# Attention's transposed exponentials in the projections' PSUM banks, and the values' eviction divided between two engines

## The chip, the core and the metric

The kernel runs on one core of a Trainium2 chip. Five engines work side by side, each through its own instructions in order, and wait for each other by semaphores: TensorE (PE), VectorE (DVE), ScalarE (ACT), GpSimd (POOL) and SyncE (SP), which issues the DMAs of the weights. Matmuls write to PSUM, which has eight banks of 512 float32 per partition; a result is brought from there to SBUF by DVE or ACT ("evicted"). The metric is the device time of one execution in microseconds, as the median of the runs; a smaller one is better.

## The reference, cut to what matters

Two transformer layers with recurrent mixers and mixtures of experts come first, and then one layer of attention and a convolutional MLP. The change touches the attention alone, which works on 256 tokens of width 1024 in 16 heads of 64:

```python
def second_block(x, ...):
    y = rms_norm_2(h, attn_norm[i])
    qkv = (y @ w_qkv[i]).reshape(B, S, 3, N_HEADS, HEAD_DIM)
    ...
    o = moba_attention(q, k, v, rel_bias)
    h = h + o.transpose(0, 2, 1, 3).reshape(B, S, D) @ w_o[i]
    y = rms_norm_2(h, ffn_norm[i])
    h = h + conv_ffn(y, ...)

def moba_attention(q, k, v, rel_bias):     # 256 tokens are one block, the block of all queries
    s_own = jnp.einsum('bhqd,bhkd->bhqk', qi, k_own) * scale
    s_own = s_own + rel_bias[:, rel_bucket(qpos[:, None] - kpos_own[None, :])]
    s_own = jnp.where(kpos_own[None, :] <= qpos[:, None], s_own, NEG)
    p = jax.nn.softmax(...)
    out = jnp.einsum('bhqk,bhkd->bhqd', p, v_own)
```

## The kernel before, in words

**Precision.** Every large float32 product is made of three products in a faster float32 format: weights and activations are split into a high and a low part (high times high, high times low, low times high; lines 346, 347 and 348 in the helper `mm3`). `split_w` makes the two parts of a piece of 128 x 1024 weights: ACT copies the high part (line 297), DVE subtracts it (line 298). Three buffers hold such pieces (`wsp`), so a piece can be split only when TensorE is done with the one three before it.

**PSUM.** The eight banks stand in two pools of four, `acc` and `aux` (lines 168 to 174). A pool hands out its banks in turn, in the order in which the program text asks for them: the fifth request waits until the bank of the first is free again.

**Attention (lines 1279 to 1355).** `proj_T` takes one `acc` bank and computes two feature tiles of q or k for all 256 tokens: 96 matmuls per pair of q and k, in four pieces of weights. The two projections of the first pair are asked for ahead (line 1279). Then the rows' root mean squares are found (`rms_rows`, ACT line 1265 and the DVE lines 454 to 464) and spread over the partitions by a matmul with ones (`rms_cols`, DVE line 1272, PE line 1274, DVE line 1275). A loop runs over four groups of four heads. In each, DVE evicts q and k (line 1300); PE computes the scores of two heads into two `aux` banks, and of two more into two others (line 1308); DVE adds the bias and finds the maxima (lines 1317, 1319); ACT takes exponentials with their sums (line 1321), DVE inverts the sums (line 1322), ACT scales (line 1324); PE transposes the three 128 x 128 blocks of each head into one `aux` bank (line 1331), and ACT or DVE copies them out (line 1334). So a group asks for two `acc` banks and eight `aux` banks.

After the loop `proj_tok` computes v in two halves of 512 columns, each as two token tiles in two `acc` banks (48 matmuls of 512 columns); ACT evicts both tiles with the rows' scale (line 1345); PE multiplies the probabilities by v (line 1352); the output projection `token_out` follows, and then the MLP, in which TensorE is busy to the end.

**Order.** The text is not the order of the engines. A scheduler sets it when the kernel is built: it takes, for each engine, the work that is free by its own estimate, and can take later work first, as far as data and the turns of the banks and buffers allow. At run time each engine keeps the order that was built.

Of the kernel before, what the change touches and what calls it, by code (L numbers as in the profile page):

```python
# [14 lines left out]
AF = mybir.ActivationFunctionType  # L15
OP = mybir.AluOpType
# [28 lines left out]
def two_layer_mixer_moe_then_attention_kernel(  # L45
# [9 lines left out]
    nc = tc.nc  # L55
# [11 lines left out]
    def slab(dt=F32):  # L67
        mem["act"] += 1
        assert mem["act"] + mem["wts"] <= SLOTS, mem
        t = big.tile([P, 2048], dt, tag="slot", name="slab")  # L70
        return t
# [4 lines left out]
    def tok(t):  # L76
        return t[:, :2048].rearrange("p (t d) -> p t d", t=2)
# [90 lines left out]
    def acc():  # L168
        b = psp.tile([P, 512], F32, tag="acc", name="acc")
        return b  # L170

    def aux():
        b = psp.tile([P, 512], F32, tag="aux", name="aux")
        return b
# [25 lines left out]
    def wa(n=512):  # L200
        return ring("a", n)
# [4 lines left out]
    def two(t):  # L206
        return t.rearrange("p (a b) -> p a b", a=2)
# [117 lines left out]
    def split_part(h, l, src):  # L325
        hi = nc.scalar.activation(h, src, AF.Copy)  # L326
        nc.vector.tensor_sub(l, src, h.bitcast(F32))  # L327
        return hi
# [38 lines left out]
    def proj_T(xh, xl):  # L367
        lo_last = len(early) > 1
        if len(early) == 1 and not tr[1:]:
            tr.append(0)  # L370
            wl_last = 1
        else:
            wl_last = 0
        ws = early.pop() if early else split_unit()
        pb = acc()
        for f in range(2):
            wh, wl = next(ws)
            o = pb[:, f * S:(f + 1) * S]
            if f < lo_last:
                mm = None  # L380
                for i, (w, x) in enumerate(((wh, xh), (wl, xh), (wh, xl))):
                    for k in range(8):
                        with tc.issue_after(mm.ins) if mm is not None else ExitStack():
                            mm = nc.tensor.matmul(o, w[:, k, :], x[:, k, :], start=i + k == 0, stop=i == 2 and k == 7)
                last[:] = [mm]
                continue
            if wl_last or lo_last:
                for k in range(8):
                    nc.tensor.matmul(o, wh[:, k, :], xh[:, k, :], start=k == 0, stop=False)
                    mm = nc.tensor.matmul(o, wh[:, k, :], xl[:, k, :], start=False, stop=False)  # L390
                for k in range(8):
                    with tc.issue_after(mm.ins):
                        mm = nc.tensor.matmul(o, wl[:, k, :], xh[:, k, :], start=False, stop=k == 7)
                last[:] = [mm]
                wl_last = 0
                continue
            for k in range(8):
                mm3(o, wh[:, k, :], wl[:, k, :], xh[:, k, :], xl[:, k, :], k == 0, k == 7)
        used()
        return pb  # L400

    def proj_tok(xh, xl):
        outs = [acc(), acc()]
        for hf in range(2):
            unit = take()
            for kp in range(2):
                wh, wl = split_w(unit[:, 2 * kp:2 * kp + 2, :])
                for k in range(2):
                    kk = 4 * hf + 2 * kp + k
                    for t in range(2):  # L410
                        mm3(outs[t], xh[:, kk, t * P:(t + 1) * P], xl[:, kk, t * P:(t + 1) * P],
                            wh[:, k, :], wl[:, k, :], kk == 0, kk == 7)
            used()
        return outs
# [846 lines left out]
    def rms_rows(h, eps=1e-6):  # L1261
        ss = tiny.tile([P, 2], F32, tag="ss", name="ss")
        y = tok(slab())
        for t in range(2):
            nc.scalar.activation(y[:, t, :], h[:, t, :], AF.Square, accum_out=ss[:, t:t + 1])
        drop()
        return [rsqrt(ss[:, t:t + 1], 1.0 / D, eps, 1) for t in range(2)]
# [12 lines left out]
    rs = rms_rows(h0)  # L1280
# [12 lines left out]
    v = tok(slab())  # L1293
    sm = tiny.tile([P, 16, 2], F32, tag="v32", name="asm", bufs=4)
    eT = []
    for a in range(4):
        qT, kT = (two(qk[:, 1024 * (a % 2) + 512 * j:1024 * (a % 2) + 512 * j + 512]) for j in range(2))
        for dst, sc in ((qT, 0.125), (kT, 1.0)):
            pb = ahead.pop(0) if ahead else proj_T(xh, xl)
            nc.vector.scalar_tensor_tensor(dst, two(pb), sc, rbb, op0=OP.mult, op1=OP.mult)  # L1300
        pes = []
        for f in range(2):
            pair = [aux(), aux()]
            for qs_, ks_, os_ in ((slice(0, 128), slice(0, 128), slice(0, 128)),
                                  (slice(128, 256), slice(0, 256), slice(128, 384))):
                for j in range(2):
                    rs_ = slice(64 * j, 64 * j + 64)
                    nc.tensor.matmul(pair[j][:, os_], qT[rs_, f, qs_], kT[rs_, f, ks_], start=True, stop=True)  # L1308
            for j in range(2):
                hi, pb = 2 * f + j, pair[j]  # L1310
                pe = wa(384)
                mx = tiny.tile([P, 2], F32, tag="amx", name="amx")
                tb = table[a // 2][:, 4 * (a % 2) + hi, :]
                rc = sm[:, 4 * a + hi, :]
                blocks = ((0, slice(0, 128), tb[:, 128:256]), (1, slice(128, 384), tb))
                for t, cs, bias in blocks:
                    nc.vector.tensor_tensor_reduce(out=pe[:, cs], in0=pb[:, cs], in1=bias, scale=1.0,
                                                   scalar=-3.0e38, op0=OP.add, op1=OP.max, accum_out=mx[:, t:t + 1])
                nc.vector.tensor_scalar(mx, mx, -1.0, None, op0=OP.mult)
                for t, cs, _ in blocks:  # L1320
                    nc.scalar.activation(pe[:, cs], pe[:, cs], AF.Exp, bias=mx[:, t:t + 1], accum_out=rc[:, t:t + 1])
                nc.vector.reciprocal(rc, rc)
                for t, cs, _ in blocks:
                    nc.scalar.activation(pe[:, cs], pe[:, cs], AF.Copy, scale=rc[:, t:t + 1])
                pes.append(pe)
        for hi in range(4):
            if len(eT) % 5 == 0:
                es = slab()
            pT = aux()
            for b in range(3):  # L1330
                nc.tensor.transpose(pT[:, b * P:(b + 1) * P], pes[hi][:, b * P:(b + 1) * P], ident)
            o = 384 * (len(eT) % 5)
            eT.append(es[:, o:o + 384])
            (nc.vector.tensor_copy if hi % 2 else nc.scalar.copy)(eT[-1], pT[:, :384])
# [7 lines left out]
    for c in range(2):  # L1342
        pbs = proj_tok(xh, xl)
        for t in range(2):
            nc.scalar.activation(v[:, t, 512 * c:512 * c + 512], pbs[t], AF.Copy, scale=rs[t])
        for a in (2 * c, 2 * c + 1):
            po = two(aux())
            for f in range(2):
                for n, r0, ks in ((0, 0, slice(0, 256)), (1, 128, slice(256, 384))):
                    for j in range(2):  # L1350
                        h = 4 * a + 2 * f + j
                        nc.tensor.matmul(po[64 * j:64 * j + 64, f, r0:], v[:, n, 64 * h:64 * h + 64], eT[h][:, ks],
                                         start=n == 0, stop=n == 1)
            split_part(uh[:, 2 * a:2 * a + 2, :], ul[:, 2 * a:2 * a + 2, :], po)
# [22 lines left out]
    pbs = [aux() for _ in range(4)]  # L1377
# [148 lines left out]
```

## Time and profile before

| | us |
|---|---|
| median of 3 runs | 1487.66 (1486.57 to 1487.93) |
| the profiled execution | 1489.95 |
| its span, first to last instruction | 1488.2 |
| PE busy in the span | 1285.9 |
| DVE busy | 551.6 |
| ACT busy | 386.9 |

The profiled execution is 0.15% above the median. The experts of the first two layers wait for their weights; the attention lies between about 1182 and 1266 us of the span, behind the last expert. A busy time is the sum of what an engine's instructions took. Matmuls overlap, so that the length of a run of matmuls is read from start to start, not from a single one's duration.

### The profile page before, as it was taken

What the parts mean: (1) busy time and instruction counts of PE and PEld (TensorE: products, weight loads), DVE (VectorE), ACT (ScalarE), POOL (GpSimd) and SP (SyncE); (2) the same over time, 40 slices, a digit from 0 to 9 for tenths busy, and PEclk for the clock granted to TensorE, in tenths of its full rate; (3) what the DMA queues carried; (4) which work ended last, traced back from release to release, by engine and by line L of the source; (5) the groups of instructions that cost most, each with busy time, mean ns of one, the idle gap of its engine ahead of it and who ended that gap; (6) DMA issues with size and microseconds to landing.
All of it is one profiled execution on the core that took longest, in us unless ns stands there. A gap on an engine that the chain in (4) does not pass through costs nothing.

```text
span 1488.2 us, 27004 instructions
## 1 busy us (share of the span) xinstructions
PE 1285.9 (86%) x11695; PEld 898.2 (60%) x11695; DVE 551.6 (37%) x1145; ACT 386.9 (26%) x637; POOL 104.5 (7%) x84
## 2 busy tenths in 40 slices
PE   9999976666667668999996769999998899999997
PEld 8887633222222226888662426656664797899996
DVE  5774211111001004886410110210100865687776
ACT  5552200000000001754210000000000467465554
POOL 1000002100100000100000210000002400010000
PEclk9999988678667789999997766876769999999999
DMA  9967999999999999847899999999999934655500
GB/s 284 374 227 293 416 420 420 421 422 421 396 421 421 420 421 358 288 172 270 340 420 421 420 413 421 420 420 421 421 421 388 357 122 136 212 191 192 178 28 29
DMA packets 129302, 492.41 MB, mean 331 GB/s; under 512 B 11570, under 2 KB 68037, under 8 KB 81056
## 3 DMA queue, kind: packets, MB, share of 16 engines
q1 hardware_dynamic: 127216, 489.93, 83.9%
q8 instruction: 92, 1.51, 0.4%
q0 software_dynamic: 864, 0.66, 0.2%
q10 hardware_dynamic: 1104, 0.10, 0.1%
q14 instruction: 26, 0.21, 0.0%
HBM read 489.61 MB, written 1.05 MB: 330 GB/s over the span
## 4 chain that ended last, share of the span: by engine, by line
PE 49%; DMA 45%; DVE 3%; POOL 1%; issue 1%; ACT 1%; SPq 0%; DVEq 0%; ACTq 0%; POOLq 0%
DMA unit<-in_moe_w_down_dram 16%; DMA unit<-in_moe_w_up_dram 15%; DMA unit<-in_moe_w_gate_dram 12%; PE acc L347 8%; PE acc L346 8%; PE acc L348 8%; PE acc L976 5%; PE aux L1220 4%; PE aux L1023 2%; PE aux L346 1%; PE aux L347 1%; PE aux L348 1%; DMA unit<-in_w_qkv_dram 1%; PE aux L1308 1%; PE aux L628 1%
## 5 line engine op out<-in xcount | busy, mean ns | idle before, releaser
L976 PE MATMUL acc<-unit,slab 128*32 128x256 f32 x3840 | 315.6, 470 | 108.2 <-DMA unit<-in_moe_w_up_dram 54.1
L976 PEld LDWEIGHTS acc<-unit,slab 128*32 128x32 f32 x3840 | 129.6, 128 | 287.9 <-DMA unit<-in_moe_w_up_dram 88.0
L347 PE MATMUL acc<-slab 128*128 128x256 f32 (+1 forms) x896 | 276.6, 309 | 1.2 <-DVE slab L327 0.8
L348 PE MATMUL acc<-slab 128*128 128x256 f32 (+1 forms) x896 | 276.1, 310 | 0.0
L346 PE MATMUL acc<-slab 128*128 128x256 f32 (+1 forms) x896 | 272.6, 310 | 2.8 <-ACT slab L326 2.8
L298 DVE TENSOR_TENSOR slab<-unit,slab 128x1024 fp32r<-128x1024 f32 x156 | 198.0, 1278 | 67.5 <-ACT slab L297 65.6
L297 ACT ACTIVATE slab<-unit 128x1024 fp32r<-128x1024 f32 x152 | 159.6, 1058 | 144.1 <-PE acc L347 73.2
L1023 PE MATMUL aux<-unit,w 128*32 128x256 f32 x1920 | 152.9, 452 | 44.0 <-DMA unit<-in_moe_w_down_dram 32.8
L346 PEld LDWEIGHTS acc<-slab 128*128 128x128 f32 x896 | 170.9, 191 | 13.7 <-ACT slab L326 3.3
L347 PEld LDWEIGHTS acc<-slab 128*128 128x128 f32 x896 | 171.2, 191 | 12.3 <-issue 2.1
L348 PEld LDWEIGHTS acc<-slab 128*128 128x128 f32 x896 | 171.6, 191 | 9.2 <-issue 1.3
L992 DVE TENSOR_TENSOR w<-w,acc 128x256 f32<-128x256 f32 x32 | 13.5, 421 | 364.2 <-PE acc L976 352.8
L1035 ACT COPY slab<-aux 32x256 f32<-32x256 f32 x60 | 21.7, 361 | 424.3 <-PE aux L1023 423.4
L1023 PEld LDWEIGHTS aux<-unit,w 128*32 128x32 f32 x1920 | 62.2, 124 | 111.2 <-DMA unit<-in_moe_w_down_dram 53.7
L1035 DVE COPY slab<-aux 32x256 f32<-32x256 f32 x60 | 25.4, 424 | 226.2 <-ACT slab L1035 225.8
L1220 PEld LDWEIGHTS aux<-slab 33*128 33x128 f32 x512 | 90.3, 272 | 13.9 <-issue 13.9
L1220 PE MATMUL aux<-slab 33*128 33x16 f32 x512 | 92.6, 328 | 0.0
L991 ACT ACTIVATE w<-acc 128x256 f32<-128x256 f32 x32 | 12.3, 383 | 275.8 <-PE acc L976 275.8
L931 PEld LDWEIGHTS aux<-slab 128*128 128x128 f32 x192 | 30.5, 204 | 8.6 <-issue 7.8
L931 PE MATMUL aux<-slab 128*128 128x128 f32 (+1 forms) x192 | 35.3, 327 | 0.0
L347 PE MATMUL aux<-slab 128*128 128x512 f32 x88 | 34.3, 390 | 0.0
L348 PE MATMUL aux<-slab 128*128 128x512 f32 x88 | 34.2, 389 | 0.0
(338 smaller groups left out, 1198.9 us busy)
## 6 DMA issues: line engine op xcount, KB each, us to landing
unit<-in_moe_w_gate_dram SPq DMA_DIRECT2D x128, 1024.0 KB, 19.8
unit<-in_moe_w_up_dram SPq DMA_DIRECT2D x128, 1024.0 KB, 19.8
unit<-in_moe_w_down_dram SPq DMA_DIRECT2D x128, 1024.0 KB, 19.8
unit<-in_w_up_dram SPq DMA_DIRECT2D x22, 1024.0 KB, 5.6
unit<-in_gla_w_in_dram SPq DMA_DIRECT2D x12, 1024.0 KB, 11.9
unit<-in_w_qkv_dram SPq DMA_DIRECT2D x12, 1024.0 KB, 11.7
unit<-in_mlstm_w_in_dram SPq DMA_DIRECT2D x11, 1024.0 KB, 13.6
unit<-in_w_down_dram SPq DMA_DIRECT2D x11, 1024.0 KB, 4.9
```

The lines of the kernel that those rows point to most:

```text
L297: nc.scalar.activation(h, src, AF.Copy)
L298: eng.tensor_tensor(l, src, h.bitcast(F32), op=OP.subtract)
L346: nc.tensor.matmul(o, ah, bh, start=first, stop=False)
L347: nc.tensor.matmul(o, ah, bl, start=False, stop=False)
L348: last[:] = [nc.tensor.matmul(o, al, bh, start=False, stop=stop)]
L628: mm = nc.tensor.matmul(o, E[d][:, h, o0:o0 + P], v[s][:, h, :], start=i == 0, stop=i == len(terms) - 1)
L931: nc.tensor.matmul(o, n_cols(t, k), ohf[:, t], start=t == 0, stop=t == 1)
L976: mm = nc.tensor.matmul(pb[32 * j:32 * j + 32, :256], picked(kk, e), unit[:, k, 256 * j:256 * j + 256], start=kk == 0, stop=kk == 7)
L1023: mm = nc.tensor.matmul(py[32 * j:32 * j + 32, :256], hT[:, kk % 2, 32 * (kk // 2):32 * (kk // 2) + 32], unit[:, k, 256 * j:256 * j + 256] ...
L1035: eng(yb[32 * eg:32 * eg + 32, g % 2, 256 * j:256 * j + 256], py[32 * j:32 * j + 32, :256])
L1220: nc.tensor.matmul(pb[:, 16 * j:16 * j + 16], cb[:, 256 - c:384 - c], relT, start=True, stop=True)
L1308: nc.tensor.matmul(pair[j][:, os_], qT[rs_, f, qs_], kT[rs_, f, ks_], start=True, stop=True)
```

## The change

The four transposes of a group go to banks of the pool `acc`, which the projections of q, k and v use, and the pool `aux` is left to the scores in this loop: a group now asks for six `acc` banks and four `aux` banks. The eviction of v is divided: the first token tile stays on ACT, the second is scaled by DVE.

```diff
@@ -1326,7 +1326,7 @@
         for hi in range(4):
             if len(eT) % 5 == 0:
                 es = slab()
-            pT = aux()
+            pT = acc()
             for b in range(3):
                 nc.tensor.transpose(pT[:, b * P:(b + 1) * P], pes[hi][:, b * P:(b + 1) * P], ident)
             o = 384 * (len(eT) % 5)
@@ -1342,7 +1342,10 @@
     for c in range(2):
         pbs = proj_tok(xh, xl)
         for t in range(2):
-            nc.scalar.activation(v[:, t, 512 * c:512 * c + 512], pbs[t], AF.Copy, scale=rs[t])
+            if t:
+                nc.vector.tensor_scalar(v[:, t, 512 * c:512 * c + 512], pbs[t], rs[t], None, op0=OP.mult)
+            else:
+                nc.scalar.activation(v[:, t, 512 * c:512 * c + 512], pbs[t], AF.Copy, scale=rs[t])
         for a in (2 * c, 2 * c + 1):
             po = two(aux())
             for f in range(2):
```

Lines behind the second edit stand three further down in the changed kernel (the product with v is line 1355). The scheduler builds another order from the changed text. On TensorE, at the scores of the first group of heads, there stood before (L1308 are scores, L346 to L348 a projection; the projection around them is the first of the third group):

```order
L346 MATMUL acc<-slab 128x256
L347 MATMUL acc<-slab 128x256
L348 MATMUL acc<-slab 128x256
L1308 MATMUL aux<-slab 128x128 x2
L1308 MATMUL aux<-slab 128x256 x2
L1308 MATMUL aux<-slab 128x128 x2
L1308 MATMUL aux<-slab 128x256 x2
L346 MATMUL acc<-slab 128x256
L347 MATMUL acc<-slab 128x256
```

And at the same scores now (L1274 spreads the root mean squares, L1331 are the transposes; the projection ahead of L1274 is the second of all, the one behind L1331 the third):

```order
L346 MATMUL acc<-slab 128x256
L347 MATMUL acc<-slab 128x256
L348 MATMUL acc<-slab 128x256
L1274 MATMUL aux<-w_8239,ones 128x128 x2
L1308 MATMUL aux<-slab 128x128 x2
L1308 MATMUL aux<-slab 128x256 x2
L1308 MATMUL aux<-slab 128x128 x2
L1308 MATMUL aux<-slab 128x256 x2
L1331 MATMUL acc<-ident,slab 128x128 x10
L346 MATMUL acc<-slab 128x256
L347 MATMUL acc<-slab 128x256
```

Ten of the twelve transposes of a group have moved up to stand right behind its scores, and the projections of the following groups, which stood between and around them, have moved behind them; the same holds in all four groups. The two last transposes stand 18 matmuls further on.

On DVE, ahead of the reductions of a group's scores (L1317, L1319), there stood before, at the first group:

```order
L298 TENSOR_TENSOR slab<-unit,slab 128x1024
L464 SCALAR_TENSOR_TENSOR rs_y<-rs_q,rs_y 128x1
L1272 TENSOR_SCALAR w_8239<-ident,rs_y 128x128
L298 TENSOR_TENSOR slab<-unit,slab 128x1024
L1275 COPY slab<-aux 128x256
L1300 SCALAR_TENSOR_TENSOR slab<-acc,slab 128x512 x3
L298 TENSOR_TENSOR slab<-unit,slab 128x1024
L1300 SCALAR_TENSOR_TENSOR slab<-acc,slab 128x512
L298 TENSOR_TENSOR slab<-unit,slab 128x1024
L1317 ISA slab,amx<-aux,slab 128x128
```

And now, at the second group (the third and the fourth are alike):

```order
L1334 COPY slab<-acc 128x384
L298 TENSOR_TENSOR slab<-unit,slab 128x1024
L1300 SCALAR_TENSOR_TENSOR slab<-acc,slab 128x512
L298 TENSOR_TENSOR slab<-unit,slab 128x1024 x2
L1300 SCALAR_TENSOR_TENSOR slab<-acc,slab 128x512
L298 TENSOR_TENSOR slab<-unit,slab 128x1024
L1317 ISA slab,amx<-aux,slab 128x128
```

The eviction of k (the second L1300) now stands one piece of weights ahead of the group's reductions instead of a group ahead of them, and the low part of a later group's weights (the last L298) stands between the two.

## Rows read from the trace of the kernel before

**Rows 1.** The page's slices: PE's busy tenths, and its granted clock in tenths.
```profile
PE   9999976666667668999996769999998899999997
PEclk9999988678667789999997766876769999999999
```

**Rows 2.** Attention's stretch: us, busy (instructions) of PE, PEld, DVE, ACT, POOL; PEclk; DMA; GB/s.
```profile
1182.10:1266.40 84.30, 81.78 (x569) 69.33 (x567) 56.17 (x155) 57.63 (x137) 9.97 (x8) 1.00 0.45 156
```

**Rows 3.** Timeline of PE, ahead of the scores: start, us, line, shapes, count, [idle before, releaser].
```profile
1176.59 0.28 PE L348 MATMUL acc<-slab 128*128 128x256 f32 x1
...
1187.39 0.28 PE L348 MATMUL acc<-slab 128*128 128x256 f32 x1
1189.03 0.49 PE L1274 MATMUL aux<-w,ones 128*128 128x128 f32 x2 [1.37 <-DVE rs_y L455]
1189.28 0.36 PE L346 MATMUL acc<-slab 128*128 128x256 f32 x1
```

**Rows 4.** Timeline of DVE, from the last root mean square to the first reductions.
```profile
1189.86 1.23 DVE L298 TENSOR_TENSOR slab<-unit,slab 128x1024 fp32r<-128x1024 f32 x1
1191.00 0.15 DVE L464 SCALAR_TENSOR_TENSOR rs_y<-rs_q,rs_y 128x1 f32<-128x1 f32 x1
1191.19 0.29 DVE L1272 TENSOR_SCALAR w<-ident,rs_y 128x128 f32<-128x128 f32 x1
...
1192.53 0.43 DVE L1275 COPY slab<-aux 128x256 f32<-128x256 f32 x1
1192.99 1.89 DVE L1300 SCALAR_TENSOR_TENSOR slab<-acc,slab 128x512 f32<-128x512 f32 x3
...
1196.85 1.22 DVE L298 TENSOR_TENSOR slab<-unit,slab 128x1024 fp32r<-128x1024 f32 x1 [0.24 <-ACT slab L297]
1198.00 0.28 DVE L1317 CUSTOM_DVE_ANT_0 slab<-aux,slab 128x128 f32<-128x128 f32 x1
...
1198.55 0.28 DVE L1317 CUSTOM_DVE_ANT_0 slab<-aux,slab 128x128 f32<-128x128 f32 x1
```

**Rows 5.** Timeline of ACT, a piece's high part and one group's exponentials.
```profile
1195.76 1.06 ACT L297 ACTIVATE slab<-unit 128x1024 fp32r<-128x1024 f32 x1 [1.81 <-PE acc L347]
...
1199.31 0.40 ACT L1321 ACTIVATE slab<-slab,amx 128x128 f32<-128x128 f32 x1 [1.18 <-DVE amx L1319]
...
1201.08 0.79 ACT L1324 ACTIVATE slab<-slab,asm 128x128 f32<-128x128 f32 x2
1201.78 1.04 ACT L297 ACTIVATE slab<-unit 128x1024 fp32r<-128x1024 f32 x1
...
1206.12 0.46 ACT L1334 COPY slab<-aux 128x384 f32<-128x384 f32 x1
```

**Rows 6.** Timeline of PE: scores, six transposes, the product with v, 512-column matmuls.
```profile
1196.85 1.58 PE L1308 MATMUL aux<-slab 64*128 64x128 f32 x16
...
1258.43 0.82 PE L1331 MATMUL aux<-ident,slab 128*128 128x128 f32 x6
...
1260.70 5.68 PE L1352 MATMUL aux<-slab 128*64 128x256 f32 x64 [1.15 <-ACT slab L1345]
...
1266.32 0.50 PE L346 MATMUL acc<-slab 128*128 128x512 f32 x1
...
1266.88 0.39 PE L348 MATMUL acc<-slab 128*128 128x512 f32 x1
...
1268.27 0.39 PE L348 MATMUL acc<-slab 128*128 128x512 f32 x1
```

**Rows 7.** Timeline of PE in the first layer, 512-column matmuls behind a wait.
```profile
105.02 0.50 PE L346 MATMUL acc<-slab 128*128 128x512 f32 x1 [2.11 <-ACT slab L326]
...
107.73 1.91 PE L348 MATMUL acc<-slab 128*128 128x512 f32 x4
109.43 0.59 PE L346 MATMUL acc<-slab 128*128 128x512 f32 x1
```

**Rows 8.** A stretch of the first layer, columns as in Rows 2.
```profile
106.45:109.86 3.41, 3.41 (x10) 2.48 (x8) 3.41 (x6) 1.22 (x3) 0.00 (x0) 0.50 1.01 425
```

## Prediction, before the changed kernel was run

> **What bounds the kernel now.** I read the page's slices first, then the attention's stretch, then single instructions in it. In the slices the reader is to see that TensorE is busy to 90% or more in nearly every slice from the last fifth of the span on, at the full clock (2.4 GHz of the two levels 1.2 and 2.4) [rows 1]. The attention lies in that part. In its 84.2 us, from the end of the second projection (1182.1) to the first matmul of the output projection (1266.3), TensorE is busy for 81.8 us, while DVE and ACT have some 27 us each to spare and the DMA is at 0.45 [rows 2]. TensorE waits there only twice: 1.37 us for the root mean squares [rows 3] and 1.15 us for ACT's eviction of v [rows 6]. So TensorE's own work bounds this stretch. The softmax of each group of heads costs no time now because projections of later groups stand between a group's scores and its transposes. Behind the attention TensorE is busy to the end, so what is lost or won here reaches the end.
>
> **The change part by part.** No instruction is added or taken away but for two evictions of v that pass from ACT to DVE. What moves is the order. The two `acc` requests of the next group's q and k now come behind four requests for transposes, and the four banks of the pool go round in turn; a projection can no longer be taken ahead of the transposes of the group before it. In the order that is built, TensorE gets scores, ten transposes, and only then the next projection, four times. Its matmuls start in order: at 1189.03 it had idled 1.37 us for one matmul, and a projection's matmul that needs nothing from that one started only behind it [rows 3]. So each softmax now stands open on TensorE. I add up the new stretch from 1182.1 on.
>
> *Wait for the root mean squares.* Matmuls of 256 columns follow each other at (1187.39 - 1176.59)/90 = 0.12 us [rows 3]; the 46 of them that still stand ahead of line 1274 end at 1182.1. Before, 105 more matmuls filled the time to the scores. Now TensorE waits. On DVE the last step of the root mean square stood behind a low part of 1.14 us (1189.86 to 1191.00), which is gone from there: it starts near 1190.0, line 1272 0.19 later, done at 1190.5; the matmul takes some 0.4 (an estimate from its 0.49 for a pair), the copy 0.46 to the next instruction, two evictions 1.89/3 = 0.63 each [rows 3, 4]. The scores start at 1192.7: **10.6 us**.
>
> *First group.* From the scores' start to the first reduction 0.95 (half of 1.58 [rows 6] and a hand-over); from there to the first exponential 0.86 (1.31 for two heads, 1198.00 to 1199.31, less one head's 0.55 and 0.1 more for the maxima taken singly [rows 4, 5]). Then ACT is the chain: up to the first block of the last head it has four heads of exponentials at (1201.08 - 1199.31)/2 = 0.885, three scalings at 0.70, half a scaling at 0.4 and one copy at 0.46 [rows 5], together 6.5. With 0.2 for the last transpose and 0.3 because these scores would run at the lower clock after the long wait: **8.8 us** to the next projection.
>
> *Groups two to four.* Each begins with 96 matmuls at 0.12 and two transposes, 11.8 us (0.82 for six [rows 6]). Then the next scores need k's eviction (0.2 and 0.68, which a group's distance hid before), and they and half of themselves would put the first reduction 1.85 us behind the projection. But the low part of a later group's weights now stands ahead of the reductions on DVE, and it needs the buffer that the last matmuls free: high part on ACT, low part on DVE, 1195.76 to 1198.00 = 2.24 [rows 4, 5], with 0.2 to release. I take 2.45, the later of the two. Then 1.31 to the first exponential for two heads, 6.5 on ACT, 0.2: 10.45 us, in which TensorE has 2.6 us of scores and transposes. Three groups of 11.8 + 10.45 make **66.7 us**.
>
> *v and the product with it.* 96 matmuls of 512 columns at (1268.27 - 1266.88)/6 = 0.232, two transposes 0.25, the product 1260.70 to 1266.32 = 5.62 [rows 6]: **28.1 us**. The eviction of v in halves costs nothing in this sum: the order puts 20 matmuls of v's second half (4.6 us) between its first half and the product, more than an eviction of some 0.65 on either engine (DVE's nearest row is 0.63 each, line 1300 [rows 4]) and a piece of weights queued ahead of it. If that cover is gone, the 1.15 us of before [rows 6] come back; it can give no more than these, and they are counted as gone already.
>
> Sum: 1182.1 + 10.6 + 8.8 + 66.7 + 28.1 = 1296.3, against 1266.3 before: **30.0 us** more. The four softmaxes and the first wait leave TensorE idle for some 40 us. Against that stand the 2.5 us of the old waits and about 7 us that the old order lost by changing between projections, scores and transposes at many places: its 84.2 us less 2.5 of waits are 81.7, and the same work in the new order adds up to 114.2 - 40 = 74.
>
> *The clock.* The trace has no wait of 7 us between bursts of full matmuls. The nearest one is 2.11 us long (to 105.02), and behind it the granted clock was 0.5 from 106.45 to 109.86 [rows 7, 8]; matmuls of 512 columns then started 1.70/4 = 0.425 us apart instead of 0.232 [rows 6, 7]. So 3.41 us at the lower level cost 3.41 x (1 - 0.232/0.425) = 1.55 us. Four bursts follow a stall here. The bounds for each are 0 (full clock when the burst starts) and the whole burst at the lower level, 11.8 us. I take 2.0, near the row and above it, since the stalls are longer than its wait: **8 us**; twice the row's, 3.1 each, is the upper end of the forecast itself. The Trainium skill, page "TensorE: Matmul & The Clock Gate", section "HAM oscillation — how this bites in real kernels", describes a kernel whose bursts of matmuls are parted by waits and which pays for the lower clock at every burst instead of once. The trace agrees as far as its one short wait goes; by that rule the four payments are made, and without it the sum ends at 1518.
>
> *Tail.* The order of transposes and splits in the first part of the MLP changes too. TensorE waits little around there before, and the same chain of evictions stays. I take 0, with -1 to +2.
>
> Forecast: 1489.95 + 30 + 8 = 1528.0 for the profiled execution. The profiled execution lies 2.29 above the median of the runs, 1487.66, so for the median 1525.7.
>
> **The rivals.**
> (a) *Stalls without the clock's price.* A stall has three transposes at a time inside, and the old waits of 1.37 and 1.15 us left the clock at full [rows 2, 3, 6]; against it speaks that a wait of 2.11 did not [rows 7, 8]. Then 1487.66 + 30 = 1517.7; with reductions that don't wait for the low part, 3 x 0.6 less, 1516.
> (b) *The clock stays low through the bursts.* Then all matmuls behind the first stall take twice their time: 3 x 11.5 + 22.2 + 5.6 = 62 us more than in (a), about 1580. Against it: in the row's stretch the clock was back at 109.86 while the same run of matmuls went on [rows 8], and these bursts are 11.5 us long.
> (c) *Faster.* Its mechanism is the unbroken order: without the changes of kind and the old waits the stretch takes 74 us instead of 84.2, a gain of 10, to 1477.7. It decides where the five stalls together are below 10 us, 2 each. That would need TensorE to take projections while transposes wait, or a softmax of a group within 2 us. Against it: the 1.37 us with work queued behind [rows 3], and ACT's 6.5 us for a group, of which nothing can be shortened by waiting less.
> (d) *The change does not do what it says*, the stalls being covered by something I don't see, and the time stays: the built order shows the opposite.
>
> **How the numbers follow.** Forecast (stalls and clock, 1519 to 1533): 0.75. (a) 1514 to 1519: 0.10. A longer sum, to 1540, with hand-overs, the clock in the scores and the tail each at their upper ends: 0.05. (b): 0.05. (c): 0.03. (d): 0.02. The predicted time is 1525.7. The range has to leave out (b), (c), (d) and may leave the outer ends of the others: 1513 to 1536. A measurement of this kernel can tell about 0.2%, 3 us, from no change. Slower by more than that are the forecast, (a), (b) and the longer sum, 0.95; within it (d), 0.02; faster (c), 0.03.
>
> **What would show it.** In the trace of the changed kernel: TensorE waits some 8 to 10 us in all ahead of the first scores, for DVE's root mean squares and evictions; in each of four groups its transposes wait for ACT's scaling (line 1324), 5 to 7 us a group, and DVE or ACT are without a gap in those stretches; the granted clock falls to 0.5 in each stall and returns within a burst; the third and fourth groups follow the second at 22 us plus the clock's price; the wait at the product with v is gone; the time from the output projection to the end is as before within 2 us. I am wrong if projections run inside the stalls, if the groups follow each other at less than 18 us, or if the loss lies behind the attention.

## The result and the profile after

The changed kernel takes **1526.56 us** (median of 5 runs, 1526.22 to 1527.51), the kernel before 1487.66 beside it (5 runs, 1485.00 to 1488.56): the ratio is 1.0258, with a 95% interval of 1.0244 to 1.0272. The change costs 39 us. The forecast was 1525.7.

The profiled execution of the kernel after took 1526.22 us, and its span is 1524.5. Its slices, as in [rows 1]: in the slices 32 to 34, which hold the attention (1181 to 1296 us here, 1153 to 1265 in the kernel before), TensorE is busy to 5, 7 and 8 tenths where the kernel before has 8, 9 and 9, and the granted clock is 7, 8 and 9 tenths instead of 9, 9 and 9.

```profile
PE   9999967676576689999977689999988578999997
PEclk9999988777768789999997758767689789999999
```

The comparison is made on TensorE, from the first matmul of line 384 (the last part of the block before) to the last matmul of all. The experts ahead of line 384 wait for their weights, and so that point moves by up to 3.7 us between runs of kernels which are the same up to there. The length behind it hardly moves with it: in acc_alone (below) that point lies 2.4 us earlier than in the kernel after, and the length is the same to 0.2 us. In the timeline of the kernel before its two ends are:

```profile
1170.52 1.67 PE L384 MATMUL acc<-slab 128*128 128x256 f32 x12 [0.87 <-DVE slab L1100]
...
1480.02 0.39 PE L348 MATMUL aux<-slab 128*128 128x512 f32 x1
```

And in the timeline of the kernel after:

```profile
1169.50 2.63 PE L384 MATMUL acc<-slab 128*128 128x256 f32 x20 [0.86 <-DVE slab L1100]
...
1516.30 0.39 PE L348 MATMUL aux<-slab 128*128 128x512 f32 x1
```

That is 309.50 us before and 346.80 after, **37.3 more**; the profiled executions differ by 36.3, since the attention of after began 1.0 us earlier.

Where the 37.3 us lie is seen in the stretches of the kernel after (columns as in [rows 2]): the wait for the root mean squares, the first group's stall, the burst of projections behind it, the second group's stall, the part of the next burst at the lower clock, and the whole from the end of the second projection to the first line behind the attention's last product.

```profile
1181.10:1192.12 11.02, 1.74 (x7) 1.04 (x5) 9.44 (x21) 4.53 (x6) 6.32 (x5) 0.64 1.02 372
1192.12:1201.33 9.21, 5.67 (x26) 3.78 (x27) 3.97 (x25) 6.67 (x25) 0.00 (x0) 0.50 0.11 46
...
1201.33:1214.60 13.27, 13.27 (x100) 13.20 (x98) 4.92 (x5) 3.74 (x5) 0.00 (x0) 0.88 0.24 80
1214.60:1224.86 10.26, 4.46 (x29) 2.64 (x27) 5.83 (x27) 7.72 (x26) 0.00 (x0) 0.84 0.25 95
1224.86:1228.50 3.64, 3.64 (x19) 3.64 (x18) 0.00 (x0) 0.56 (x2) 0.00 (x0) 0.50 0.05 19
...
1181.10:1306.40 125.30, 95.51 (x585) 79.37 (x583) 63.75 (x161) 61.59 (x139) 10.04 (x8) 0.84 0.32 109
```

The stretch of [rows 2] was 84.2 us long and is now 125.3, of which 3.9 belong elsewhere: 17 of the 96 matmuls of the output projection now stand ahead of the last product (17 x 0.232 [rows 6]). So it grew to 121.4, by 37.2. From there to the end the time is the same to 0.1 us.

The timeline of TensorE shows the stalls one by one: the end of the second projection, the spread of the root mean squares, scores and transposes of the first group, the next projection, and the same for the second group. The third is alike; in the fourth two other small matmuls (lines 1338 and 1339) start inside the stall and part its wait of 3.30 us into 0.48 and 2.30.

```profile
1180.97 0.28 PE L348 MATMUL acc<-slab 128*128 128x256 f32 x1
1187.92 0.80 PE L1274 MATMUL aux<-w,ones 128*128 128x128 f32 x2 [6.67 <-DVE rs_y L455]
1189.39 0.79 PE L1274 MATMUL aux<-w,ones 128*128 128x128 f32 x2 [0.67 <-DVE w L1272]
1192.12 2.93 PE L1308 MATMUL aux<-slab 64*128 64x128 f32 x16 [1.93 <-DVE slab L1300]
1196.86 1.78 PE L1331 MATMUL acc<-ident,slab 128*128 128x128 f32 x6 [1.81 <-ACT slab L1324]
1200.38 1.30 PE L1331 MATMUL acc<-ident,slab 128*128 128x128 f32 x4 [1.73 <-ACT slab L1324]
1201.33 0.56 PE L346 MATMUL acc<-slab 128*128 128x256 f32 x1
...
1214.45 0.28 PE L348 MATMUL acc<-slab 128*128 128x256 f32 x1
1215.52 1.58 PE L1308 MATMUL aux<-slab 64*128 64x128 f32 x16 [0.78 <-DVE slab L1300]
1220.40 0.84 PE L1331 MATMUL acc<-ident,slab 128*128 128x128 f32 x3 [3.30 <-ACT slab L1324]
1221.47 1.09 PE L1331 MATMUL acc<-ident,slab 128*128 128x128 f32 x3 [0.24 <-ACT slab L1324]
1223.91 1.30 PE L1331 MATMUL acc<-ident,slab 128*128 128x128 f32 x4 [1.34 <-ACT slab L1324]
1224.86 0.56 PE L346 MATMUL acc<-slab 128*128 128x256 f32 x1
```

The same matmul of line 1274 that had waited 1.37 us [rows 3] now ends 6.67 us of idleness, and each set of transposes waits for ACT's scaling. The sums over the attention are in the table of TensorE's waits of the kernel after (us in total, times, longest):

```profile
PE acc L1331 <- ACT slab L1324: 17.3, 11, 3.3
PE aux L1274 <- DVE rs_y L455: 6.7, 1, 6.7
PE aux L1308 <- DVE slab L1300: 4.3, 4, 1.9
```

What holds the reductions of the second group back is on DVE, as in [rows 4]: k's eviction (line 1300), then the low part of a later group's weights (line 298), then the reductions (line 1317).

```profile
1214.77 0.69 DVE L1300 SCALAR_TENSOR_TENSOR slab<-acc,slab 128x512 f32<-128x512 f32 x1 [0.68 <-PE acc L348]
1215.74 1.23 DVE L298 TENSOR_TENSOR slab<-unit,slab 128x1024 fp32r<-128x1024 f32 x1 [0.28 <-ACT slab L297]
1216.88 0.28 DVE L1317 CUSTOM_DVE_ANT_0 slab<-aux,slab 128x128 f32<-128x128 f32 x1
```

And the end of the attention: the first projection of v behind the fourth stall, at the lower clock until 1276.29, and the product with v (line 1355, which was line 1352 in [rows 6]), now without a wait ahead of it.

```profile
1272.34 0.78 PE L346 MATMUL acc<-slab 128*128 128x512 f32 x1
...
1276.31 0.39 PE L346 MATMUL acc<-slab 128*128 128x512 f32 x1
...
1290.08 2.82 PE L1355 MATMUL aux<-slab 128*64 128x256 f32 x32
...
1306.40 0.50 PE L346 MATMUL acc<-slab 128*128 128x512 f32 x1
```

### The profile page after: what moved, and what is told of

Same layout as the page of the kernel before. It is cut to its first block, busy times and chain, and to the rows that moved or that the text cites. A ratio compares the mean times of both kernels' runs of the same rounds, so it can differ in the third digit from the quotient of the medians.

```text
span 1524.5 us, 27009 instructions
## 1 busy us (share of the span) xinstructions
PE 1291.9 (85%) x11695; PEld 904.0 (59%) x11695; DVE 554.2 (36%) x1147; ACT 387.0 (25%) x635; POOL 105.1 (7%) x84
## 4 chain that ended last, share of the span: by engine, by line
PE 47%; DMA 44%; DVE 4%; ACT 2%; POOL 1%; issue 1%; SPq 0%; DVEq 0%; ACTq 0%; POOLq 0%
DMA unit<-in_moe_w_down_dram 16%; DMA unit<-in_moe_w_up_dram 15%; DMA unit<-in_moe_w_gate_dram 12%; PE acc L347 8%; PE acc L346 8%; PE acc L348 8%; PE acc L976 5%; PE aux L1220 4%; PE aux L1023 2%; PE aux L346 1%; PE aux L347 1%; PE aux L348 1%; ACT slab L1321 1%; PE aux L628 1%; PE aux L186 1%
## 5 line engine op out<-in xcount | busy, mean ns | idle before, releaser
L346 PE MATMUL acc<-slab 128*128 128x256 f32 (+1 forms) x896 | 275.7, 313 | 2.9 <-ACT slab L326 2.4
L348 PE MATMUL acc<-slab 128*128 128x256 f32 (+1 forms) x896 | 277.0, 311 | 0.0
L298 DVE TENSOR_TENSOR slab<-unit,slab 128x1024 fp32r<-128x1024 f32 x156 | 198.2, 1278 | 87.7 <-ACT slab L297 84.6
L346 PEld LDWEIGHTS acc<-slab 128*128 128x128 f32 x896 | 173.9, 194 | 12.5 <-ACT slab L326 2.9
L347 PEld LDWEIGHTS acc<-slab 128*128 128x128 f32 x896 | 173.8, 194 | 10.4 <-issue 1.1
L348 PEld LDWEIGHTS acc<-slab 128*128 128x128 f32 x896 | 173.6, 194 | 8.7 <-issue 0.8
L348 PE MATMUL aux<-slab 128*128 128x512 f32 x88 | 34.2, 389 | 0.0
```

The costliest lines, as they stand in the source:

```text
L298: eng.tensor_tensor(l, src, h.bitcast(F32), op=OP.subtract)
L346: nc.tensor.matmul(o, ah, bh, start=first, stop=False)
L347: nc.tensor.matmul(o, ah, bl, start=False, stop=False)
L348: last[:] = [nc.tensor.matmul(o, al, bh, start=False, stop=stop)]
```

## The experiments

The theory: a pool hands its banks out in the order of the text; with the transposes' requests in `acc` a projection can't pass the transposes that stand ahead of it there, TensorE stands idle through each softmax, and the idleness is paid for a second time by the lower clock. The rivals: the four banks of `acc` are simply too few for six requests a group; the clock's price is nil and the stalls are longer in its place; the eviction of v by DVE has a part in it. Each kernel was run beside the kernel before, and the ratios are formed with those runs (medians of the kernel before: 1487.23 for the first four experiments, 1487.94 for the last three); they differ by up to 0.001 from the quotient of the medians. Lengths in the profile are from the first matmul of line 384 to the start of the last matmul, taken as above:

| kernel | median, us | ratio to before (95%) | profile: length, us | against before |
|---|---|---|---|---|
| before | 1487.66 | | 309.50 | |
| after | 1526.56 | 1.0258 (1.0244 to 1.0272) | 346.80 | +37.3 |
| v_halves | 1488.44 | 1.0001 (0.9991 to 1.0010) | 309.26 | -0.2 |
| acc_alone | 1523.17 | 1.0235 (1.0218 to 1.0253) | 347.01 | +37.5 |
| one_in_acc | 1513.00 | 1.0162 (1.0143 to 1.0180) | 333.55 | +24.1 |
| warm_stalls | 1517.80 | 1.0197 (1.0176 to 1.0219) | 339.58 | +30.1 |
| next_first | 1498.83 | 1.0068 (1.0054 to 1.0083) | 318.77 | +9.3 |
| two_ahead | 1485.51 | 0.9984 (0.9974 to 0.9994) | 306.40 | -3.1 |
| two_ahead_aux | 1487.60 | 0.9998 (0.9988 to 1.0007) | 307.94 | -1.6 |

**The two edits apart.** v_halves is the kernel before with the second edit alone:

```diff
-            nc.scalar.activation(v[:, t, 512 * c:512 * c + 512], pbs[t], AF.Copy, scale=rs[t])
+            if t:
+                nc.vector.tensor_scalar(v[:, t, 512 * c:512 * c + 512], pbs[t], rs[t], None, op0=OP.mult)
+            else:
+                nc.scalar.activation(v[:, t, 512 * c:512 * c + 512], pbs[t], AF.Copy, scale=rs[t])
```

> The kernel before with v's eviction divided between ACT and DVE, and nothing else. Theory (the loss is the order that the transposes' banks force): the old order stays, no stall appears, and at most the 1.15 us that TensorE waited for ACT's four evictions go: 1486.5 to 1487.7. Rival (DVE's share of the eviction delays the splits of weights that queue behind it on DVE): over 1490.

It takes the time of before to 0.1%, by the ratio; its median lies 0.7 us above the expected range and well below the rival's. The 1.15 us at the product, which the second edit might have taken away, stayed. ACT's timeline in v_halves shows why (line 1348 is the eviction of v there, line 1355 the product):

```profile
1258.13 1.06 ACT L297 ACTIVATE slab<-unit 128x1024 fp32r<-128x1024 f32 x1 [2.05 <-PE acc L348]
1259.10 0.46 ACT L1334 COPY slab<-aux 128x384 f32<-128x384 f32 x1
1259.46 1.27 ACT L1348 ACTIVATE slab<-acc,rs_y 128x512 f32<-128x512 f32 x2
```

And TensorE's:

```profile
1260.20 5.42 PE L1355 MATMUL aux<-slab 128*64 128x256 f32 x64 [1.15 <-ACT slab L1348]
```

The product waits for the first eviction of v. That one stays on ACT, behind the high part of a piece of weights and a copy of transposes; only evictions behind it passed to DVE, and for those the product did not wait.

acc_alone is the first edit alone:

```diff
-            pT = aux()
+            pT = acc()
```

> The kernel before with the transposes in the projections' banks, and nothing else. Theory: the whole loss, 1525.5 to 1528. Rival (the divided eviction of v carries part of it): below 1522.

It carries the whole loss: 347.0 us in the profile against 346.8 with both edits, and waits of TensorE in the attention that are those of after to 0.1 us:

```profile
PE acc L1331 <- ACT slab L1324: 17.4, 11, 3.3
PE aux L1274 <- DVE rs_y L455: 6.7, 1, 6.7
PE aux L1308 <- DVE slab L1300: 4.3, 4, 1.9
```

Its median is 3.4 us below that of after and 2.3 below what was expected. Its profiled execution is 2.2 us shorter than that of after, and line 384 starts 2.4 us earlier in it (1167.08): that difference lies ahead of the attention, and no part of the loss passes to the second edit.

**Order or number of banks.** In one_in_acc only the first of a group's four transposed heads asks for an `acc` bank, so that a group has three requests there for four banks:

```diff
-            pT = acc()
+            pT = aux() if hi else acc()
```

> The changed kernel, with only the first of a group's four heads transposed in the projections' banks, the other three in the old ones. Theory: the next projection has to stand behind the first transpose alone, so a stall ends at that head's first scaled block, 2.2 us after the first exponential instead of 6.4; the wait ahead of the first scores stays; 1526.6 less 4 x 4.2 is 1510, and 1506 to 1514 with the clock and the changes of kind. Rival (a price for each transpose in those banks, whatever the order): a quarter of the loss, 1497.

While the scores of a group are on their way, q and k of that group have been evicted, and one bank at most waits for a head: there are free banks for the next projection. It waits all the same. TensorE's timeline of one_in_acc at the second group:

```profile
1213.22 1.58 PE L1308 MATMUL aux<-slab 64*128 64x128 f32 x16 [0.78 <-DVE slab L1300]
1218.10 0.33 PE L1331 MATMUL acc<-ident,slab 128*128 128x128 f32 x1 [3.30 <-ACT slab L1324]
1218.18 0.36 PE L346 MATMUL acc<-slab 128*128 128x256 f32 x1
```

The wait of 3.30 us up to the first scaled block is that of after; with that head's first transpose started, the projection starts 0.08 us behind it, and the other heads' transposes stand among the projections. The median of one_in_acc lies within the expected range, 16 us above the rival's. So one request in the shared pool makes 24 of the 37 us, and the other three add 13. The order of requests is shown as a cause by itself; how far the last three heads cost by their order or by keeping all four banks full was not separated.

**The clock's price.** In warm_stalls TensorE multiplies ones in the stalls, with results that nobody reads:

```diff
     ahead = [proj_T(xh, xl) for _ in range(2)]
+    warm(12, last[0])
...
             pT = acc()
+            if hi % 2 == 0:
+                warm(2 if hi else 6, sc, pT[:, :S])
```

(`warm(n, i, t)` puts a chain of n products of 256 columns behind instruction i, into the bank t; `sc` is the last matmul of the scores.)

> The changed kernel with matmuls of ones added that nobody reads: 12 ahead of the first scores, and in each group 6 behind the scores and 2 between the transposes, where TensorE waits. Theory: the granted clock stays at full through the stalls, and the half-clock matmuls behind each go; the trace of the changed kernel has 3.3, 3.6, 3.9 and 4.0 us of projections at half clock, 6.5 us lost, and 1.3 in the first scores and sums: 1518 to 1520. Rival (the clock's price lies inside the waits and costs nothing): 1526 to 1528.

The stalls stay as long as they were: from the end of a projection to the next, at the second group, 10.0 us (1211.75 to 1221.70) against 10.1 (1214.73 to 1224.86). What changes is the speed behind them. In these stretches of warm_stalls the clock is low once, in the first group, and at 1.00 from there on:

```profile
1189.62:1196.45 6.83, 6.16 (x24) 4.71 (x25) 3.74 (x24) 3.16 (x14) 0.00 (x0) 0.50 0.27 104
1196.45:1300.00 103.55, 95.61 (x631) 80.34 (x630) 52.45 (x120) 55.29 (x124) 3.31 (x3) 1.00 0.30 93
```

The gain is 7.2 us in the profile (346.8 to 339.6). The medians differ by 8.8, which puts that of warm_stalls 0.2 us below the expected range; of the 8.6 between the profiled executions 1.4 lie ahead of line 384 (1168.07 against 1169.50). The clock's price is real, and near the 8 us of the forecast.

**The order undone while the banks stay shared.** next_first keeps the transposes in `acc`, but its text asks for the next group's q and k ahead of them:

```diff
+    coming = q_and_k(0)
     for a in range(4):
-        qT, kT = (two(qk[:, 1024 * (a % 2) + 512 * j:1024 * (a % 2) + 512 * j + 512]) for j in range(2))
-        for dst, sc in ((qT, 0.125), (kT, 1.0)):
-            pb = ahead.pop(0) if ahead else proj_T(xh, xl)
-            nc.vector.scalar_tensor_tensor(dst, two(pb), sc, rbb, op0=OP.mult, op1=OP.mult)
+        qT, kT = coming
...
+        if a < 3:
+            coming = q_and_k(a + 1)
         for hi in range(4):
             pT = acc()
```

(`q_and_k(a)` holds the removed lines.)

> The changed kernel, same banks, with the projections and evictions of the next group's q and k written in the text ahead of a group's transposes. Theory (the text's order of requests makes the loss, not the banks): the wait ahead of the first scores shrinks to the 1.4 us of before, the second and third group's softmax are covered by projections; the first and the fourth group's still stand open (4 and 8 us, with 1.7 us each for the clock): 1492 to 1499. Rival (transposes in the projections' banks cost this by themselves): 1520 to 1527.

28 of the 37 us are back; the median lies within the expected range, at its upper end. (The lines of the attention stand some lines further down in this kernel: 1313 are the scores, 1322 the reductions, 1329 ACT's scaling, 1338 the transposes.) What is left lies in the first group, where scores wait for banks that reductions still read (line 1322), and in the fourth, which has no projection of q and k behind it. From TensorE's timeline of next_first:

```profile
1198.46 0.92 PE L1313 MATMUL aux<-slab 64*128 64x128 f32 x4 [0.77 <-DVE amx L1322]
1200.36 0.92 PE L1313 MATMUL aux<-slab 64*128 64x128 f32 x4 [0.98 <-DVE amx L1322]
...
1239.65 2.16 PE L1338 MATMUL acc<-ident,slab 128*128 128x128 f32 x6 [2.31 <-ACT slab L1329]
1243.15 1.30 PE L1338 MATMUL acc<-ident,slab 128*128 128x128 f32 x4 [1.35 <-ACT slab L1329]
```

**Two groups ahead.** two_ahead goes on: the text stands two groups ahead, with the halves of v in the place of the projections that the last two groups lack.

```diff
+    coming = [q_and_k(0), q_and_k(1)]
     for a in range(4):
-        qT, kT = (...)
+        qT, kT = coming.pop(0)
...
+        if a < 2:
+            coming.append(q_and_k(a + 2))
+        else:
+            values(a - 2)
         for hi in range(4):
             pT = acc()
```

(`values(c)` is the eviction of v by halves of the changed kernel, moved up.)

> The same with the text two groups ahead: the projections of group a+2 (for the last two groups, v's halves) ahead of group a's transposes. Theory: no softmax stands open, the clock stays at full, and the unbroken order saves part of the 7 us that the old order lost by changing between kinds of matmuls: 1478 to 1485, below the kernel before. Rival (the unbroken order saves nothing, the old one's losses come back elsewhere): 1486 to 1489.

All waits for the softmax are gone, and with them the dips of the clock. It is 0.16% faster than the kernel before, 0.06 to 0.26% by the interval: the only version whose interval lies below the kernel before, by 2.4 us between the medians of runs made side by side and 3.1 in the profile. The expected range, which hoped for more, was missed by 0.5 us. The attention's stretch in it answers to that of [rows 2]:

```profile
1180.24:1261.27 81.03, 79.66 (x568) 68.46 (x567) 58.62 (x157) 56.55 (x136) 10.29 (x8) 1.00 0.45 158
```

And TensorE's waits in that stretch are one:

```profile
PE aux L1274 <- DVE rs_y L455: 1.4, 1, 1.4
```

two_ahead_aux is the same text with the transposes in `aux` again (`pT = aux()`).

> The same text with the transposes back in the banks of the scores. Theory: projections were never bound to the transposes there, so no stall either; the next scores are bound to the transposes' start again, and changes of kind come back in part: 1480 to 1487, between the other and the kernel before. Rival (the projections' banks are worse for the transposes in any order): clearly below the other by over 2 us.

It takes the time of before, 0.6 us above the expected range. The rival is excluded, since it is not faster than two_ahead. Its timeline has one wait that two_ahead lacks (line 1348 are the transposes there, line 1337 ACT's scaling):

```profile
1258.12 0.33 PE L1348 MATMUL aux<-ident,slab 128*128 128x128 f32 x1 [1.64 <-ACT slab L1337]
```

In that text the change's banks are thus no loss but a small gain, 2.1 us between the medians and 1.5 in the profile, about the size of that wait. That is near the limit of what these runs tell apart, and the two intervals overlap; it is taken as likely, not as shown.

## Why the prediction was right, step by step

The forecast of 38 us had the right sum by the right parts, with one part 1.5 us too large. Each term against the trace of after:

| term | predicted, us | measured, us | from |
|---|---|---|---|
| wait for the root mean squares | 10.6 | 11.0 | 1181.10 to 1192.12 |
| first group | 8.8 | 9.2 | 1192.12 to 1201.33 |
| groups two to four, at full clock | 66.7 | 66.3 | 1201.33 to 1272.34 less 4.7 for the clock |
| v and the product, at full clock | 28.1 | 28.3 | 1272.34 to 1306.40 less 3.9 of the output projection and 1.8 for the clock |
| clock, behind the four stalls | 8 | 6.5 | below |
| tail | 0 | +0.1 | 213.70 to 213.84, from the output projection's start, corrected by the 3.9 |

Together the measured terms make 37.2 us. That the sum came out so close is in part luck: the clock's term was 1.5 too large, and the first two were 0.8 too small. The medians differ by 38.9; the 1.6 us beyond the 37.3 of the profile belong to no term of the sum, and are less than the 3.7 us by which the start of line 384 moves.

**Order on TensorE.** Right. The built order was the whole argument: ten transposes right behind the scores, at every group. Experiments acc_alone and one_in_acc show it as the cause.

**Root mean squares.** 0.4 us over. DVE was as early as forecast (the second line 1272 at 1189.05, which is 1190.07 in the time of before, against 1190.2 forecast). The miss is on TensorE: the pairs of line 1274 took 0.80 us instead of 0.49 [rows 3], because the clock was already low there. The forecast had put the clock's price into the scores only.

**First group.** 0.4 over, for the same reason: its scores took 2.93 us at the lower clock instead of 1.58 [rows 6], so that the first reduction began 1.65 us behind their start (1192.12 to 1193.77), where 0.95 and 0.3 for the clock were forecast. From the first exponential (1194.66) on ACT set the pace as forecast, 6.67 us to the next projection against 6.7; that the transposes between took longer too (1.78 us for six instead of 0.82) cost nothing.

**The later groups.** The mechanism was seen in the right place. Each of the three stalls took 10.29 us (in the second group 1214.45 to 1224.86, less 0.12 for the projection's last matmul), where 10.45 was forecast. DVE did the low part between k's eviction and the reductions, and these began 2.31 us behind the projection's end (1214.45 and 0.12, to 1216.88), where 2.45 was forecast. The first exponential followed 1.31 us later, at 1218.19, as in [rows 4, 5]. The scores of the groups start 23.4, 23.7 and 23.8 us apart, 22.2 and the clock's share. One sign was put too high: I expected the transposes to wait for line 1324 for 5 to 7 us a group, and it is 4.9 in the second (3.30, 0.24 and 1.34), 17.3 in all four; more of the stall than I thought is taken by scores and transposes themselves.

**v in halves.** Costs nothing, as forecast, by v_halves and by after less acc_alone. The wait of 1.15 us at the product is gone in after, but by the new order: v_halves shows that the halves alone leave it, and acc_alone, which has the new order without the halves, doesn't have it either.

**The clock.** Forecast 4 x 2.0 = 8; behind the stalls the projections ran at the lower level for 3.28, 3.64, 3.85 and 3.95 us. Matmuls of 256 columns then stand 0.214 us apart instead of 0.12 (1201.69 to 1201.90 and on), those of 512 columns 0.427 instead of 0.232, so the price is 1.44, 1.60, 1.69 and 1.80, together 6.5, near the 1.55 of the short wait of [rows 7, 8] in spite of stalls more than four times as long. What the clock cost in line 1274 and in the first scores stands in the first two rows of the table. warm_stalls, which has the four bursts at full clock, gains these 6.5 and some 0.7 in the waits and stalls. The page "TensorE: Matmul & The Clock Gate" of the Trainium skill (section "HAM oscillation — how this bites in real kernels") has the lower clock paid at every burst behind a wait, and this trace agrees: four stalls, four payments of 1.4 to 1.8 us.

**The step that failed.** It is not in the sum, which goes from start to start: it is the work that an unbroken order saves, and the rival of the faster outcome rested on it. I had put 7 us down to changes between kinds of matmuls, as the difference of 81.7 and 74 us of work, where the 74 came from some 40 us of idleness: the first wait and the stalls, less 2.6 us of scores and transposes in each stall. TensorE was idle for 29.8 us only (125.30 less 95.51, in the stretch of after): scores and transposes in short runs, some at the lower clock, kept it busy for 4.46 us in the second group's stall. With 30 us in the place of 40 nothing is left of the 7: 114.2 less 30 is more than 81.7. two_ahead is that order without the stalls: 39 runs of one kind in the stretch (projection, scores, transposes, product and so on) against 77 before, and 79.66 us of work against 81.78 [rows 2]. That is 2.1 us. With the old wait of 1.15 it makes 3.3 in the stretch and most of the 3.1 us that two_ahead gains, where rival (c) had 10.

Not every change costs the same. In the trace of before, the first scores start 0.21 us behind the last matmul of a projection (1196.64 to 1196.85), and the next projection 0.31 behind the last score (1198.05 to 1198.36), against 0.12 within a projection; a lone transpose among its matmuls adds only 0.11 (from the matmul at 1203.02 over the transpose to the second matmul behind, at 1203.37, it is 0.35, where two steps alone are 0.24). So it is the way to the scores and back that costs, some 0.3 us by these numbers. Since two_ahead has 9 runs of scores where before has 13, that would be about half of the 2.1 us, as an estimate; no experiment parts it from the rest.

**The other rivals.** Without the clock's price (a) had 30.0 us more than before; warm_stalls, which is nearly that case made, has 30.1 in the profile. A clock that stays low through the bursts (b) is excluded by the rows of after: 1.00 returns 3.3 to 4.0 us into each. Too few banks, the rival of the experiments, is not enough: the page "Perfetto Trace Analysis" of the Trainium skill (section "Optimization Strategy") reads a repeated gap on the engine that should be saturated as a possible sign of too few buffers in PSUM. Here a gap of 3.30 us stands in the second and third groups, and it stays at 3.30 in one_in_acc, which has a bank to spare; the remedy that worked was another order of requests (next_first, two_ahead).

## What to carry to other kernels

A pool that hands out banks in turn, in the order of the text, works as a queue in the order that is built: whoever asks in it stands behind everyone who asked earlier, ready or not. Before work that waits for another engine is given banks of the pool that feeds TensorE, look in the built order at what stands behind that work; if it must share, ask for the independent work first, a whole latency ahead. Each stall of 9 to 11 us on a saturated TensorE counted twice here, with its own length and with 1.4 to 1.8 us for the lower clock behind it. Matmuls whose results nobody reads bought back the second part (warm_stalls); the first came back only with another order of requests (next_first, two_ahead).

## What the runs showed of the hardware

In the second to fourth groups more than half of the time at the lower clock falls on the work behind the stall. In the second group the stall began at 1214.6, with scores and transposes in it, and the clock was at 1.00 until 1221.68; it was then 0.50 for 6.8 us, more than half of it in the burst. Stretches of the kernel after:

```profile
1184.13:1204.61 20.48, 10.54 (x45) 8.10 (x46) 10.57 (x43) 10.02 (x30) 3.29 (x4) 0.50 0.44 164
...
1214.60:1221.68 7.08, 2.69 (x22) 1.61 (x20) 4.94 (x24) 4.54 (x15) 0.00 (x0) 1.00 0.00 0
...
1221.68:1228.50 6.82, 5.41 (x24) 4.66 (x24) 0.89 (x3) 3.74 (x13) 0.00 (x0) 0.50 0.41 154
```

The first row is the long one: a wait of 6.67 us and then scores and transposes with gaps of 0.67 to 1.93 us between them, and the clock came back 3.28 us into the projection behind them. In the second row TensorE had 2.69 us of scores and transposes, and the clock fell at its end. The price behind a stall, on the other hand, hardly depended on its length in these cases: 1.55 us behind a wait of 2.11 [rows 7, 8], 1.4 to 1.8 behind stalls of 9 to 11. The clock also fell behind short waits: in next_first it did so after two waits of 0.77 and 0.98 us among the first group's scores, and TensorE was busy all through the 6.83 us at the lower level, while the 1.37 and 1.15 us of the kernel before left the clock at 1.00 [rows 2, 3, 6]. A stretch of next_first:

```profile
1201.49:1208.32 6.83, 6.83 (x29) 5.79 (x29) 3.86 (x25) 6.83 (x26) 0.00 (x0) 0.50 0.00 0
```
